# Gate products as quarter-array tiles, and three channel pairs of the output projections in float32

## The chip, the cores and the metric

The kernel runs on one core of one Trainium2 chip. The metric is the device time of one execution in microseconds (us), as the median of the runs made. Three runs of the kernel before gave 1067.7, 1067.75 and 1068.0 us. A profile holds one further execution, seen by the hardware profiler. The engines are called by short names: PE (TensorE, the matrix engine; PEld is its weight loading), DVE (VectorE), ACT (ScalarE), POOL (GpSimd) and SP (SyncE, which here issues the loads).

## What is computed

A decoder trunk of four layers on 256 tokens of width 1024, all in float32. Layers 0 and 3 mix tokens with an RG-LRU recurrence, layer 1 with a spatial gating unit, layer 2 with a short convolution, and after each of them stands a squared-ReLU MLP. The change touches the RG-LRU mixer alone:

```python
gate, xr = jnp.split(h @ w_in, 2, axis=-1)
gate = jax.nn.gelu(gate)
xr = _causal_dwconv(xr, conv_w) + conv_b
xh = xr.reshape(b, s, A_HEADS, A_HEAD_DIM)          # 16 heads of 80 channels
r = jax.nn.sigmoid(jnp.einsum("bshi,hij->bshj", xh, gate_a_w).reshape(b, s, D_RNN) + gate_a_b)
ig = jax.nn.sigmoid(jnp.einsum("bshi,hij->bshj", xh, gate_x_w).reshape(b, s, D_RNN) + gate_x_b)
log_a = -LRU_C * r * jax.nn.softplus(-lam)
a = jnp.exp(log_a)
u = jnp.sqrt(-jnp.expm1(2.0 * log_a)) * (ig * xr)
_, hs = lax.associative_scan(_lru_combine, (a, u), axis=1)
return (hs * gate) @ w_out
```

The two gates r and ig are block products: each of the 16 heads multiplies its 80 channels by its own 80 x 80 matrix, once for each gate. D_RNN is 1280, so the channels fill ten tiles of 128.

## The kernel before

Activations lie with channels on the 128 partitions and the 256 tokens along the free axis. Weights stream from memory in chunks of 128 x 2048 values, in two raw loads of 128 x 1024 (`fetch`, lines 152 to 181).

**Split products.** A large product isn't done in float32. The raw weights are cast on ACT to a rounded part `whi` (L176), DVE subtracts that from the raw ones to get `wlo` (L179), the moving side is split in the same way, and `mm3` (L240 to L243) issues three products per 128 x 128 block of weights: high by high, high by low, low by high. A few products are done in float32 from the raw weights instead, with no cast and no subtraction; the profile shows each of those as two matmul instructions. A chunk for float32 is called whole.

**The mixer of layers 0 and 3** (`class Mixer`). The program calls them layer 0 and layer 1 of this mixer, and so does this text: first mixer and second mixer. PE's order of work is `tensor_steps`, which goes through `LRU_ORDER`: the ten tiles of the recurrent branch, the ten tiles of the gated branch, and two groups of gate products ("gates", 0 and 1) between them. Then comes the output projection, five pairs of channel tiles of 32 split products' worth each (2 tiles x 8 output tiles, 48 matmuls), in the order 0 to 4 into four accumulator banks (L604 to L624). For one pair, (mixer 0, pair 1), `UNSPLIT` (L88) says that it is done in float32: two whole chunks, the recurrence output `hs` itself as moving side, L618.

The order of ACT and DVE is written out by hand in `LRU_STEPS` (L66). A word P lets PE's program run on to its next yield; C and S pop the next cast and subtraction of a weight chunk; any other word is a method of `Mixer` with a tile or pair number: x and K, k (branch and convolution), r (both gates of a tile: tanh on ACT, L714), e (exponentials, L726), da, db, dc, u, v, w, a (DVE arithmetic), s (square root, L747), z (scan, L762), g and G (gated branch and its gelu, L768 and L772), m (product of both, L776), i and o (high and low part of the result, L780 and L785). ACT and DVE work in exactly this order, each as soon as its inputs are there. PE takes an operand when it is ready and else waits with all that is behind it.

**The gates before** (`gate_steps`, L626 to L663). One group is five channel tiles with eight heads. The channels are ordered (`_rnn_order`) so that four tiles hold one whole head of 80 and 48 channels of a second one, and the fifth, called hub, holds the 4 x 32 channels left over. In one group PE does, in float32: the own product of each of the five tiles for each gate, ten of 128 x 128 (L646); the hub's share into the four tiles, 32 rows each, eight products, four of them on different row quarters of the array (L654, the tile position is the row); and the four tiles' share into the hub, eight products of 32 columns, four on different column quarters (L661). Both gates of one tile lie in one PSUM bank, so a group takes five of the eight banks. Line 714 then reads a gate of a tile in one instruction.

```python
for m in (*tiles, hub):
    banks[m] = bank().rearrange("p (j t) -> p j t", t=T)
    for e in range(2):
        nc.tensor.matmul(banks[m][:, e, :], block(), self.tile_of(m), start=e == 0, stop=False,
                         skip_group_check=True)
```

`_band_chunks` (L1038) lays the weights of a group out as 14 blocks of 128 x 128, in the order in which PE uses them, in two whole chunks of eight and six.

## Time and profile before

| | |
|---|---|
| median of three runs | 1067.75 us (1067.7 to 1068.0) |
| the profiled execution's own time | 1068.12 us |
| its span, from the first to the last instruction | 1066.1 us |
| PE busy | 1059.1 us, 99% |
| DVE busy | 725.8 us, 68% |
| ACT busy | 587.0 us, 55% |
| POOL busy | 52.5 us, 5% |
| read from memory | 200.94 MB, 189 GB/s over the span |

The span is what the trace shows; the 2.0 us between it and the execution's own time lie around it. Busy time is what instructions of an engine occupy, so for PE, whose matmuls overlap, it says only that something was under way. Start times of successive instructions tell its pace. The trace can be asked for groups of instructions by line, for one engine's instructions in order of time, for the waits, and for the chain of work that ended last.

### The profile page before, as it was taken

The numbers are of one execution on the slowest core, as the hardware profiler recorded it, in microseconds if no ns is written. First come the engines' busy times: TensorE is split into PE (matmuls) and PEld (weight loads), VectorE is DVE, ScalarE is ACT, GpSimd is POOL, SyncE is SP. The second block draws the span as 40 slices with busy tenths as digits, with TensorE's granted clock in tenths as the row PEclk, the third lists the DMA queues.
The fourth block names the chain that finished last, engine by engine and source line by source line (L and its number), as shares of the span: only waits on it lengthen the run. The fifth ranks groups of instructions, "written<-read, shape, count | busy, mean of one in ns | idle before, by whom it ended". The sixth has DMA issues, their size and how long they took to land.

```text
span 1066.1 us, 21817 instructions
## 1 busy us (share of the span) xinstructions
PE 1059.1 (99%) x9158; PEld 1046.8 (98%) x9158; DVE 725.8 (68%) x970; ACT 587.0 (55%) x819; POOL 52.5 (5%) x167
## 2 busy tenths in 40 slices
PE   9999999999999999999999999999999999999997
PEld 9999999999999999999999999999999999999997
DVE  7999765555758575555777766555578997755553
ACT  7697554454574464445544455445456975644442
POOL 3400100000210100000010010000010001000000
PEclk9999999999999999999999999999999999999999
DMA  9666585655646386665466447565554545866401
GB/s 334 254 238 213 174 279 190 194 195 190 205 162 215 98 293 196 192 194 194 155 223 198 161 138 279 195 192 189 190 179 157 175 155 181 293 192 195 131 1 41
DMA packets 58706, 203.40 MB, mean 191 GB/s; under 512 B 6640, under 2 KB 8304, under 8 KB 58608
## 3 DMA queue, kind: packets, MB, share of 16 engines
q1 hardware_dynamic: 58176, 201.49, 56.5%
q8 instruction: 72, 1.18, 0.5%
q10 hardware_dynamic: 432, 0.52, 0.1%
q14 instruction: 26, 0.21, 0.1%
HBM read 200.94 MB, written 1.05 MB: 189 GB/s over the span
## 4 chain that ended last, share of the span: by engine, by line
PE 97%; issue 2%; DVE 0%; ACT 0%; POOLq 0%; POOL 0%
PE ps L242 90%; PE ps L812 2%; PE ps L646 2%; PE ps L618 1%; PE ps L248 0%; PE ps L654 0%; PE ps L661 0%; PE ps L848 0%; PE ps L323 0%; PE ps L353 0%; DVE u L452 0%; POOLq L1139 0%; DVE lo L457 0%; POOL o L945 0%; ACT hi L454 0%
## 5 line engine op out<-in xcount | busy, mean ns | idle before, releaser
L179 DVE TENSOR_TENSOR wlo<-raw,whi 128x1024 fp32r<-128x1024 f32 (+1 forms) x378 | 440.6, 1197 | 219.5 <-ACT whi L176 219.4
L242 PE MATMUL ps<-xs,whi 128*128 128x256 f32 x3200 | 548.5, 277 | 0.0
L176 ACT CAST whi<-raw 128x1024 fp32r<-128x1024 f32 (+1 forms) x378 | 374.1, 1030 | 310.0 <-issue 286.5
L242 PEld LDWEIGHTS ps<-xs,whi 128*128 128x128 f32 x3200 | 482.9, 188 | 1.3 <-issue 0.4
L242 PE MATMUL ps<-xs,wlo 128*128 128x256 f32 x1600 | 442.0, 276 | 0.0
L242 PE MATMUL ps<-hi,whi 128*128 128x256 f32 x1296 | 357.9, 276 | 0.0
L242 PE MATMUL ps<-hi,wlo 128*128 128x256 f32 x1296 | 357.7, 276 | 0.0
L242 PE MATMUL ps<-lo,whi 128*128 128x256 f32 x1296 | 357.7, 276 | 0.0
L242 PEld LDWEIGHTS ps<-xs,wlo 128*128 128x128 f32 x1600 | 300.7, 188 | 0.0
L242 PEld LDWEIGHTS ps<-hi,whi 128*128 128x128 f32 x1296 | 243.3, 188 | 0.0
L242 PEld LDWEIGHTS ps<-lo,whi 128*128 128x128 f32 x1296 | 243.3, 188 | 0.0
L242 PEld LDWEIGHTS ps<-hi,wlo 128*128 128x128 f32 x1296 | 243.3, 188 | 0.0
L452 DVE SCALAR_TENSOR_TENSOR u<-ps,rs 128x512 f32<-128x512 f32 x64 | 44.0, 687 | 45.6 <-PE ps L242 33.2
L454 ACT ACTIVATE hi<-u 128x512 fp32r<-128x512 f32 x64 | 40.3, 630 | 16.5 <-DVE u L452 16.5
L457 DVE TENSOR_TENSOR lo<-hsq,hi 128x512 fp32r<-128x512 f32 x64 | 44.0, 688 | 4.5 <-ACT hsq L455 2.4
L281 ACT ACTIVATE xs<-x,cst 128x256 fp32r<-128x256 f32 x64 | 29.1, 501 | 30.8 <-DVE x L410 29.1
L307 POOL TENSOR_SCALAR rc<-rc 128x2 int32<-128x2 int32 x9 | 9.6, 1069 | 682.0 <-ACT rc L306 682.0
L455 ACT ACTIVATE hsq<-u 128x512 f32<-128x512 f32 x64 | 39.4, 616 | 0.0
L282 DVE SCALAR_TENSOR_TENSOR xs<-x,cst,xs 128x256 fp32r<-128x256 f32 x64 | 28.5, 480 | 12.2 <-ACT xs L281 12.2
L340 DVE TENSOR_SCALAR diag<-eye,rc 128x128 fp32r<-128x128 f32 x32 | 7.2, 285 | 29.4 <-POOL rc L330 29.4
L702 DVE SCALAR_TENSOR_TENSOR xc<-xr,cst,xc 128x255 f32<-128x255 f32 (+2 forms) x60 | 24.0, 474 | 0.0
L301 DVE TENSOR_TENSOR sum<-sum,sq 128x256 f32<-128x256 f32 x52 | 21.8, 420 | 1.4 <-ACT sq L428 0.6
(123 smaller groups left out, 478.7 us busy)
## 6 DMA issues: line engine op xcount, KB each, us to landing
raw<-weights SPq DMA_DIRECT2D x369, 512.0 KB, 4.3
raw<-first SPq DMA_DIRECT2D x16, 256.0 KB, 4.6
raw<-weights SPq DMA_DIRECT2D x4, 384.0 KB, 6.8
x<-xT SPq DMA_DIRECT2D x8, 128.0 KB, 4.4
sb<-sbias SPq DMA_DIRECT2D x2, 256.0 KB, 5.1
outT<-o SPq DMA_DIRECT2D x1, 256.0 KB, 2.1
outT<-o ACTq DMA_DIRECT2D x1, 256.0 KB, 2.1
outT<-o SPq DMA_DIRECT2D x2, 128.0 KB, 2.5
```

The costliest lines, as they stand in the source:

```text
L176: return nc.scalar.copy(out=hi[:, s], in_=raw[:, e])
L179: return nc.vector.tensor_tensor(out=lo[:, s], in0=raw[:, e], in1=hi.bitcast(F32)[:, s], op=SUB)
L242: nc.tensor.matmul(ps, a, b, start=start and n == 0, stop=stop and n == 2, skip_group_check=True)
L281: nc.scalar.activation(xs[:, hi], x, AF.Copy, scale=g)
L282: nc.vector.scalar_tensor_tensor(out=xs[:, lo], in0=x, scalar=g, in1=xs.bitcast(F32)[:, hi], op0=MULT, op1=SUB)
L301: nc.vector.tensor_tensor(out=sq_now[0], in0=sq_now[0], in1=sq[:, j, :], op=ADD)
L452: yield nc.vector.scalar_tensor_tensor(out=u, in0=ps, scalar=0.0, in1=both(scale.row), op0=MAX, op1=MULT)
L454: yield nc.scalar.activation(hi, u, AF.Square)
L455: yield nc.scalar.activation(sq, u, AF.Square)
L457: yield nc.vector.tensor_tensor(out=lo, in0=sq, in1=hi.bitcast(F32), op=SUB)
L646: nc.tensor.matmul(banks[m][:, e, :], block(), self.tile_of(m), start=e == 0, stop=False, skip_group_check=True)
L702: return [nc.vector.scalar_tensor_tensor(out=c[:, j, d:], in0=x[:, j, :T - d], scalar=self.tap(3 - d, 2 * i + j), in1=c[:, j, d:], op0=MUL ...
```

## The change

The 1280 channels are put in another order: the four tiles of a group now hold 64 channels of each of two heads (the two in the two halves of the partitions), and the hub holds the last 16 of each of the eight heads. With that an own product of one tile falls into two 64 x 64 products for each gate. The program issues the four of both gates one behind the other, on the four quarters of the array: the products of the first gate (e = 0) on the diagonal, from rows h to the same half of the output partitions, those of the second gate off it, so that the second gate's output halves lie swapped. Two tiles share two PSUM banks, one bank for each position e; a group still takes five banks. The eight products from the hub come in two parts of four, with e's bank exchanged for every second tile so that the four go to four banks. Between the two parts lie all of the hub's own products: they are now 4 x 32 columns for each gate (eight products side by side in fours), then the four tiles' share as before (eight). The second part waits for a one-element memset on POOL, `passed`, which itself waits for the first part's last product. On ACT, r now reads the second gate of the four tiles in two halves of 64 partitions, to undo the swap. A group's weights are 10 blocks in place of 14, in chunks of eight and two.

Beside that, pair 2 of the first mixer and pair 1 of the second are now done in float32 as well: three whole pairs instead of one. Their C, S, i and o steps go. In the first mixer the second group of gates now comes behind two more gated tiles, and both step lists are written anew.

```diff
--- before.py
+++ after.py
@@ -46,14 +46,14 @@
-SHARE = P // 4
+HALF, SHARE = P // 2, P // 4
 LRU_ORDER = (
     (
         ("branch", 8), ("branch", 2), ("gated", 4), ("gates", 0),
-        ("gates", 1), ("gated", 2), ("gated", 4),
+        ("gated", 2), ("gates", 1), ("gated", 4),
     ),
     (
         ("branch", 4), ("branch", 2), ("branch", 4), ("gates", 0),
@@ -64,18 +64,17 @@
 LRU_STEPS = (
...
+    "P8 na P nv P3 C P S C P S C P S C nd P C S P C S nb P S nr x0 P x1 K0 x2 P K1 x3 k0 P K2 C P k1 C P K3 P C "
+    "k2 C P C P S C x4 P C S K4 P k3 C P2 k4 P g0 P g1 r4 S P r3 S P r0 S r1 P S r2 P u0 e0 S P g2 P S e1 P da0 "
+    "u1 db0 da1 P dc0 P db1 s0 dc1 s1 P v0 v1 w0 P G0 a0 r6 w1 P z0 r8 a1 P m0 r9 z1 i0 P r7 o0 P u4 r5 u3 P G1 "
+    "u2 m1 P g3 e2 g4 P e3 P da2 db2 P dc2 e4 da3 P db3 dc3 da4 P db4 s2 dc4 s3 P v2 v3 w2 P G2 a2 w3 C z2 a3 m2 "
+    "s4 z3 P S G3 P C m3 G4 v4 i3 S P C o3 C P w4 C a4 S C P z4 C P S C P m4 C S i4 P C o4 S P C S C P S P2",
     "P4 C P C P S C S na P nv S C P S P2 C P S C nd P S nb C P nr S C P x0 P x1 K0 x2 K1 S P K2 k0 P C P C k1 P2 "
...
+    "k2 P2 x3 P x4 K3 S K4 k3 P r4 P r2 k4 P r3 r0 P S r1 P u1 C P u0 C g0 P S P S e1 P C da1 P db1 r5 S P r6 dc1 "
+    "P u2 e0 P C P da0 db0 S P s1 dc0 P s0 v1 v0 P w1 G0 w0 r8 a0 P a1 z0 C P g1 C m0 P G1 z1 i0 r7 P o0 m1 r9 P "
+    "g2 S P e2 u3 S P u4 e3 P da2 db2 P dc2 e4 g3 da3 P g4 db3 P da4 dc3 db4 s2 P s3 dc4 C v2 P v3 s4 w2 a2 P w3 "
+    "G2 z2 C P a3 G4 m2 G3 z3 P i2 C o2 m3 C P S i3 P C v4 o3 C P w4 C a4 S P C z4 P C S C P m4 S i4 P o4 P S S P "
+    "C S C P2 S P",
 )
@@ -85,7 +84,7 @@
-UNSPLIT = (0, 1)
+UNSPLIT = ((0, 1), (0, 2), (1, 1),)
 def _const_columns():
@@ -187,6 +186,12 @@
         tc.add_manual_dep(ins, other.name,
                           mybir.DependencyInfo(mybir.DependencyClass.NoSync, mybir.DependencyReason.DATA),
+                          reason="order")
+    def wait_for(ins, other):
+        tc.add_manual_dep(ins.ins, other.ins.name,
+                          mybir.DependencyInfo(mybir.DependencyClass.Sync, mybir.DependencyReason.DATA),
                           reason="order")
     def chain():
@@ -603,7 +608,7 @@
                             yield
             self.acc = [bank() for _ in range(KD // 2)]
             for i in range(KR // 2):
-                whole_pair = (self.layer, i) == UNSPLIT
+                whole_pair = (self.layer, i) in UNSPLIT
                 if whole_pair:
                     raws = [next_chunk() for _ in range(2)]
                 else:
@@ -627,6 +632,8 @@
             at, w = 0, None
             def block():
@@ -640,26 +647,50 @@
             tiles = range(g * GRP, hub)
             banks = self.banks["gates"]
-            for m in (*tiles, hub):
-                banks[m] = bank().rearrange("p (j t) -> p j t", t=T)
+            def banks_of(ms):
+                two = [bank().rearrange("p (j t) -> p j t", t=T) for _ in range(2)]
+                for i, m in enumerate(ms):
+                    banks[m] = [two[e][:, i, :] for e in range(2)]
+            for i, m in enumerate(tiles):
+                if i % 2 == 0:
+                    banks_of(tiles[i:i + 2])
+                b, x = block(), self.tile_of(m)
                 for e in range(2):
-                    nc.tensor.matmul(banks[m][:, e, :], block(), self.tile_of(m), start=e == 0, stop=False,
-                                     skip_group_check=True)
-                if m in (tiles[1], hub):
+                    for h in range(2):
+                        k, c = (slice(n * HALF, (n + 1) * HALF) for n in (h, h ^ e))
+                        nc.tensor.matmul(banks[m][e][c], b[k, c], x[k], start=i % 2 == 0, stop=False,
+                                         tile_position=(h * HALF, (h ^ e) * HALF), skip_group_check=True)
+                if i % 2:
                     yield
-            for e in range(2):
+            def from_fifth(e, ended=None):
                 b = block()
                 for i, m in enumerate(tiles):
                     q = slice(i * SHARE, (i + 1) * SHARE)
-                    nc.tensor.matmul(banks[m][:, e, :], b[q], self.tile_of(hub)[q], start=False, stop=True,
-                                     tile_position=(i * SHARE, 0), skip_group_check=True)
+                    mm = nc.tensor.matmul(banks[m][e ^ (i % 2)], b[q], self.tile_of(hub)[q], start=False, stop=True,
+                                          tile_position=(i * SHARE, 0), skip_group_check=True)
+                    if ended is not None and i == 0:
+                        wait_for(mm, ended)
+                return mm
+            seen = work.tile([1, 1], F32, name="seen", tag="seen")
+            wave = from_fifth(0)
+            passed = nc.gpsimd.memset(seen, 0.0)
+            wait_for(passed, wave)
+            ps = bank().rearrange("p (j t) -> p j t", t=T)
+            banks[hub] = [ps[:, e, :] for e in range(2)]
+            for own in (True, False):
+                for e in range(2):
+                    b = block()
+                    for i, m in enumerate(tiles):
+                        q = slice(i * SHARE, (i + 1) * SHARE)
+                        nc.tensor.matmul(banks[hub][e][q], b[:, q], self.tile_of(hub if own else m),
+                                         start=own and e == 0, stop=not own, tile_position=(0, i * SHARE),
+                                         skip_group_check=True)
             yield
-            for e in range(2):
-                b = block()
-                for i, m in enumerate(tiles):
-                    q = slice(i * SHARE, (i + 1) * SHARE)
-                    nc.tensor.matmul(banks[hub][q, e, :], b[:, q], self.tile_of(m), start=False, stop=True,
-                                     tile_position=(0, i * SHARE), skip_group_check=True)
+            from_fifth(1, passed)
             yield
         def tile_of(self, m):
@@ -711,8 +742,10 @@
             made = []
             for e, dst in enumerate((self.rg, self.ig)):
                 c = (2 * e + self.layer) * KR + m
-                made.append(nc.scalar.activation(dst[m // 2][:, m % 2, :], self.banks["gates"][m][:, e, :], AF.Tanh,
-                                                 scale=0.5, bias=half_b[:, c:c + 1]))
+                out, ps = dst[m // 2][:, m % 2, :], self.banks["gates"][m][e]
+                for h in ((slice(0, HALF), slice(HALF, P)) if e and m % GRP < GRP - 1 else (slice(0, P),)):
+                    there = h if h.stop - h.start == P else slice(HALF - h.start, P - h.start)
+                    made.append(nc.scalar.activation(out[h], ps[there], AF.Tanh, scale=0.5, bias=half_b[h, c:c + 1]))
             return made
@@ -1029,28 +1062,32 @@
     out = []
     for g in range(D_RNN // (GRP * P)):
         heads = [np.arange((g * 8 + h) * HEAD, (g * 8 + h + 1) * HEAD) for h in range(8)]
-        for i in range(GRP - 1):
-            out += [heads[i], heads[GRP - 1 + i][:P - HEAD]]
-        out += [heads[GRP - 1 + i][P - HEAD:] for i in range(GRP - 1)]
+        out += [h[:HALF] for h in heads] + [h[HALF:] for h in heads]
     return np.concatenate(out)
 def _band_chunks(gates, g):
-    own, to_four, to_fifth = [], [], []
+    own, to_four, last, to_fifth = [np.zeros((P, P), np.float32) for _ in range(GRP - 1)], [], [], []
     order = _rnn_order()[g * GRP * P:(g + 1) * GRP * P] - g * GRP * P
-    for w in gates:
+    parts = [slice(i * SHARE, (i + 1) * SHARE) for i in range(GRP - 1)]
+    halves = [slice(0, HALF), slice(HALF, P)]
+    for e, w in enumerate(gates):
         full = np.zeros((GRP * P, GRP * P), w.dtype)
         for h in range(GRP * P // HEAD):
             s = slice(h * HEAD, (h + 1) * HEAD)
             full[s, s] = w[g * GRP * P // HEAD + h]
         tiles = full[order][:, order].reshape(GRP, P, GRP, P)
-        parts = [slice(i * SHARE, (i + 1) * SHARE) for i in range(GRP - 1)]
-        own.append([tiles[m, :, m] for m in range(GRP)])
-        to_four.append(np.concatenate([tiles[-1, q, i] for i, q in enumerate(parts)], axis=0))
+        for m in range(GRP - 1):
+            for h in range(2):
+                own[m][halves[h], halves[h ^ e]] = tiles[m, halves[h], m, halves[h]]
+        to_four.append([np.roll(tiles[-1, q, i], e * HALF, axis=1) for i, q in enumerate(parts)])
+        last.append(tiles[-1, :, -1])
         to_fifth.append(np.concatenate([tiles[i, :, -1, q] for i, q in enumerate(parts)], axis=1))
-    cols = [b for pair in zip(*own) for b in pair] + to_four + to_fifth
+    rows = [np.concatenate([to_four[e ^ (i % 2)][i] for i in range(GRP - 1)]) for e in range(2)]
+    cols = own + rows[:1] + last + to_fifth + rows[1:]
     return [np.concatenate(cols[i:i + 8], axis=1) for i in range(0, len(cols), 8)]
@@ -1075,7 +1112,7 @@
                     out += _in_chunks(w, at[what], at[what] + arg * P, arg * P)
                     at[what] += arg * P
             for n, c in enumerate(_out_chunks(p["a_w_out"][j])):
-                out += unsplit([c[:, :D], c[:, D:]]) if (j, n) == UNSPLIT else [c]
+                out += unsplit([c[:, :D], c[:, D:]]) if (j, n) in UNSPLIT else [c]
         elif kind == "b":
             w = p["b_w_in"][j]
             out += _in_chunks(w, D, 2 * D) + _in_chunks(w, 0, D)
```

## Rows read from the trace of the kernel before

**Rows 1.** The page's first part, PE and DVE and ACT and POOL in one line (busy us, share of the span, instructions), and below it all the waits of PE that the trace puts down to another engine (total us, times, longest).

```profile
PE 1059.1 (99%) x9158; PEld 1046.8 (98%) x9158; DVE 725.8 (68%) x970; ACT 587.0 (55%) x819; POOL 52.5 (5%) x167
...
PE ps L248 <- DVE ones L253: 1.1, 1, 1.1
PE ps L938 <- DVE diag L935: 0.4, 1, 0.4
```

**Rows 2.** Groups of PE's instructions by line and shape over the whole run (weights rows*columns, moving shape, count | busy us, mean ns of one | idle before).

```profile
L646 PE MATMUL ps<-xc,raw 128*128 128x256 f32 x80 | 18.0, 380 | 0.0
...
L654 PE MATMUL ps<-xc,raw 32*128 32x256 f32 x64 | 4.6, 400 | 0.0
L661 PE MATMUL ps<-xc,raw 128*32 128x256 f32 x64 | 4.3, 385 | 0.0
```

**Rows 3.** Two pieces of the chain that ended last, in order of time: start us, length us, line and count of matmuls. The first is output projection in float32, the second a stretch with split products alone.

```profile
80.55 6.91 PE ps L618 x32
...
365.60 167.30 PE ps L242 x1476
```

**Rows 4.** PE in order of time across both gate groups of the first mixer: start us, us until the last of them ends, line, shapes, count.

```profile
45.44 4.48 PE L646 MATMUL ps<-xc,raw 128*128 128x256 f32 x20
49.85 1.15 PE L654 MATMUL ps<-xc,raw 32*128 32x256 f32 x16
50.92 1.07 PE L661 MATMUL ps<-xc,raw 128*32 128x256 f32 x16
51.92 4.58 PE L646 MATMUL ps<-xc,raw 128*128 128x256 f32 x20
56.44 1.15 PE L654 MATMUL ps<-xc,raw 32*128 32x256 f32 x16
57.51 1.07 PE L661 MATMUL ps<-xc,raw 128*32 128x256 f32 x16
58.51 0.51 PE L242 MATMUL ps<-xs,whi 128*128 128x256 f32 x2
```

**Rows 5.** The same for narrow windows at the start of the four-row-quarter products of the first group, up to 50.14 and then up to 50.20 us: how many had started.

```profile
49.85 0.50 PE L654 MATMUL ps<-xc,raw 32*128 32x256 f32 x4
...
49.85 0.71 PE L654 MATMUL ps<-xc,raw 32*128 32x256 f32 x8
```

**Rows 6.** PE in order of time around the first gate group of the second mixer, where the split products go on behind it.

```profile
813.67 4.48 PE L646 MATMUL ps<-xc,raw 128*128 128x256 f32 x20
818.08 1.15 PE L654 MATMUL ps<-xc,raw 32*128 32x256 f32 x16
819.15 1.07 PE L661 MATMUL ps<-xc,raw 128*32 128x256 f32 x16
...
820.15 0.50 PE L242 MATMUL ps<-xs,whi 128*128 128x256 f32 x2
```

**Rows 7.** POOL in order of time, two of its instructions on 128x2 values: the usual length and the longest.

```profile
795.26 0.20 POOL L311 TENSOR_TENSOR rc<-rc 128x2 f32<-128x2 f32 x1
...
798.34 1.25 POOL L311 TENSOR_TENSOR rc<-rc 128x2 f32<-128x2 f32 x1
```

**Rows 8.** ACT in order of time in the first mixer: start us, us, line, operation, count. Loads of a function table stand as ACT_TABLE_LOAD.

```profile
51.01 0.47 ACT L714 ACTIVATE rg<-ps,half_b 128x256 f32<-128x256 f32 x1 [5.89 <-PE ps L654]
51.38 0.47 ACT L714 ACTIVATE ig<-ps,half_b 128x256 f32<-128x256 f32 x1
...
54.59 1.15 ACT L726 ACTIVATE q<-rg,lam 128x256 f32<-128x256 f32 x2
55.58 1.14 ACT L726 ACTIVATE rg<-rg,lam 128x256 f32<-128x256 f32 x2
...
64.23 1.28 ACT L747 ACT_TABLE_LOAD   x1
65.52 1.15 ACT L747 ACTIVATE rg<-rg 128x512 f32<-128x512 f32 x2
66.69 1.28 ACT L772 ACT_TABLE_LOAD   x1
```

**Rows 9.** DVE in order of time in the first mixer, up to the finished pair 2 (its product with the gate is L776, its low part L785), and three subtractions of weights that follow each other.

```profile
81.16 0.42 DVE L758 TENSOR_SCALAR q<-q 128x512 f32<-128x512 f32 x1
81.50 0.68 DVE L751 SCALAR_TENSOR_TENSOR rg<-q,rg 128x512 f32<-128x512 f32 x1
82.10 1.26 DVE L762 TENSOR_TENSOR_SCAN rg<-q,ig 128x256 f32<-128x256 f32 x2
83.28 0.66 DVE L754 TENSOR_TENSOR ig<-ig,rg 128x512 f32<-128x512 f32 x1
83.86 0.68 DVE L776 TENSOR_TENSOR rg<-rg,gate 128x512 f32<-128x512 f32 x1
...
85.94 0.68 DVE L785 TENSOR_TENSOR lo<-rg,hi 128x512 fp32r<-128x512 f32 x1
...
97.36 3.48 DVE L179 TENSOR_TENSOR wlo<-raw,whi 128x1024 fp32r<-128x1024 f32 x3
100.77 0.68 DVE L410 TENSOR_TENSOR x<-ps,x 128x512 f32<-128x512 f32 x1
```

**Rows 10.** PE in order of time where the projection of pair 2 of the first mixer begins, behind the float32 products of pair 1.

```profile
87.11 0.47 PE L242 MATMUL ps<-hi,whi 128*128 128x256 f32 x1
```

11 rows, old and new, of the table LRU_STEPS are left out of this document.

## The prediction

> **What bounds the kernel now.** I read the page's busy times first, then PE's waits. PE is busy for 1059.1 of 1066.1 us, and all its waits for other engines are 1.5 us, at the very start and at the very end [rows 1]. Between those two ends nothing stops PE. So its time is a sum of matmuls, and an edit is worth what it takes from that sum, as long as ACT and DVE still deliver in time. Busy time can't give the price of a matmul, since they overlap: the groups show a mean of 380 ns for one of L646 [rows 2], yet twenty of them start within 4.41 us [rows 4]. So I price by starts, and by pieces of the chain divided by their count.
>
> **Prices.** A split product takes 167.30 / 1476 = 0.1133 us, a full float32 instruction 6.91 / 32 = 0.216 us [rows 3]. Instructions on different quarters of the array go side by side: after 49.85 us four start at once and the next four at about 50.17 [rows 5], and sixteen need 1.07 us [rows 4], four waves, against 16 x 0.216 = 3.45 us one by one.
>
> A change of shape costs extra. Twenty full products are 20 x 0.2155 = 4.31 us and the next shape starts after 4.41: 0.10 us for leaving. The second group's twenty need 4.52, 0.11 more, because they are entered from another shape [rows 4]. Four waves are 0.86 us; the 32-row stage takes 1.07, so 0.21 for entering and leaving, the 32-column stage 1.00, so 0.14 [rows 4]. With 0.105 for each leaving, entering is 0.105 for 32 rows and 0.03 for 32 columns.
>
> **The gates before.** One group is 4.41 + 1.07 + 1.00 us, with 0.11 for entering what follows: 6.59 us. The second mixer has the same 6.48 from 813.67 to 820.15, before that 0.11 [rows 6].
>
> **The gates after.** In waves of four instructions, each product being two instructions:
> - own products: 4 tiles x 4 quarters x 2 = 32 instructions, 8 waves
> - from the hub, first part: 4 x 2 = 8, 2 waves
> - the hub's own in 32 columns (8 x 2) and the four tiles' share (8 x 2): 8 waves
> - from the hub, second part: 2 waves
>
> That is 20 waves, 4.31 us. Shapes change five times in place of three: five leavings at 0.105 are 0.53, enterings are 0.105 twice, 0.03, 0.11 and one into 64 x 64, which the trace doesn't have. Its bounds are the neighbours, 0.03 and 0.11; I take 0.07, as 64 columns lie between 32 and 128. Sum 0.53 + 0.42 = 0.95, and a group is 5.26 us: 1.33 less, 5.3 us over four groups. If one wave could not hold four, it would be worse; a wave of all four quarters fills the array, so nothing makes it cheaper.
>
> No row shows four quarters of 64 x 64. The nearest rows are the two kinds of four side by side, by rows and by columns, both at about 0.215 a wave. The dear end is one by one as in L646. I take the cheap end because both halves of the new shape, separate row groups and separate column groups, run side by side in the rows; the next part prices the rest.
>
> **The float32 pairs.** A split pair is 48 x 0.1133 = 5.44 us, a float32 pair 32 x 0.216 = 6.91. Two more of them cost 2 x 1.47 = 2.9 us on PE. This is certain: pair 1 of the first mixer does it already.
>
> **What the other engines get.** Each such pair takes two weight subtractions from DVE, 1.14 us each (three in 100.77 - 97.36), and one o of 0.6, so 2.9 us, and from ACT two casts and one i. The gates' extra half reads give ACT 8 more instructions a mixer, 0.37 us each [rows 8], 2.9 us. The first mixer's new list also puts s4 between G2 and G3, so two more table loads of 1.3 us there [rows 8]. DVE is relieved, ACT a little more loaded, and neither sets the end by its sum. Loads shrink by four blocks a group, 1 MB in all; PE waits for no load now, so I count nothing.
>
> **The new wait.** The second hub part waits for POOL, which waits for the first part. Behind it on PE stands everything. Its cover is the hub stage between them, 8 waves and one change, 1.8 us. POOL's small instructions take 0.20 us, at worst 1.25 [rows 7]. A hand-over is short: the products of L654 end at 49.85 + 1.15 = 51.00 and ACT, which waits for them, starts at 51.01 [rows 4, 8]. With 0.1 us for two of them (my estimate from that) the wait is over after 0.3 to 1.4 us. I count nothing; with the cover gone it would cost up to 1.4 us four times.
>
> **The place without reserve.** In the first mixer the second gate group moves behind two gated tiles, so PE asks for pair 2 sooner after it. PE's clock: gates from 45.44, 5.26 us; two gated tiles 5.44; gates 5.26; four gated tiles 96 x 0.1133 = 10.9; pair 0 5.44; pair 1 6.91: pair 2 at 84.6 us. Before it was at 87.1 [rows 10], and its low part was ready at 86.6 [rows 9]. Now it needs only m2. ACT can begin r at about 49.9, when the hub stage ends. Up to s3 it has 28 gate reads (10.0 us), twenty e (9.9 at 0.495), four s and two G (6 x 0.55 = 3.3), one i (0.5), and four table loads (5.2), 28.9 us [rows 8], with about 0.8 us of gaps where s1 and i0 wait for DVE: 79.6. v can begin 0.5 earlier, after s2. Then DVE has v2, v3, w2, a2, w3, z2, a3, m2: five at 0.6, two at 0.34 and 1.18, and 0.08 until the last is through, 4.9 us [rows 9]: m2 is ready at about 84.0 to 84.5. It is 84.6 that counts: just in time. I take no stall, and keep 0 to 1.5 us for the range. The second mixer keeps its order of stages, and its pair 1 now takes PE 1.5 us longer, about what its gates save, so its pairs are asked for at nearly the old times and I count no wait there.
>
> **Sum.** -5.3 + 2.9 = -2.4 us. The profiled execution's 1068.12 us (span 1066.1 and 2.0 around it) becomes 1065.7; the median of the runs is 0.37 below that execution, so 1065.4 us.
>
> **The rivals.**
>
> *PSUM banks keep the quarters apart (slower).* The two products of one gate come from different row halves and go to the same bank, on different partitions. In the rows four row quarters write four banks (L654, a bank for each tile), and four column quarters one bank from the same rows (L661); one bank from two row halves at once is not among them. If these are held apart, a wave holds two instructions, own products need 16 waves in place of 8, 1.72 us more a group, 6.9 in all, and the kernel ends at 1065.4 + 6.9 = 1072.3 us. It decides as soon as a wave of own products takes more than 0.36 us: 32 such waves less 2.4 us are even. One by one, 24 more waves a group, it would be 20.7 us more. For it: such a form is nowhere in the trace. Against it: the partitions differ, and in L661 column quarters share a bank without loss.
>
> The Trainium skill speaks for this rival: TensorEngine Tiling (Array Packing), Restrictions and Gotchas, says under PSUM Pressure that different row tiles go to different banks and can't access the same bank at the same time. By that rule the own products would go by twos and the sum would be the rival's. The trace of before keeps to the rule everywhere, so it can't tell whether the rule holds for separate partitions too.
>
> *Pair 2 comes late (a wait for ACT or DVE takes the place of the matmuls).* If ACT runs 0.5 to 2 us behind my sum, PE stands before pair 2 of the first mixer for 0.5 to 1.5 us, and nothing behind it makes that good: 1065.9 to 1066.9, say 1066.3. For it: no reserve, two more table loads, longer gate reads. Against it: what ACT does can be added up from the rows, and the same lists now run without one wait.
>
> *The POOL wait shows.* With 1.4 us against a cover of 1.8 it doesn't. If the hand-overs and the memset took 2.1 us together, it would be 0.3 us four times, 1066.6.
>
> **How the numbers follow.** The forecast, 1065.0 to 1065.9, has 0.65; pair 2 or the POOL wait late 0.20; banks or one by one 0.15. The range 1064.7 to 1067.3 holds the first two. 0.2% of 1067.75 is 2.1 us, about what a measurement of this kernel can tell from no change, and the forecast of -2.4 lies just beyond it: of the forecast's 0.65 I give 0.47 to faster and 0.18 to same. Late cases are same, with a little for faster; slower is the bank case. Faster 0.48, same 0.38, slower 0.14.
>
> **What would show it.** Right: PE's own products of a group in starts of four, 0.215 us apart, and 1.9 us from their first start to the next shape; 1.8 us for the hub stage; 6.9 us for each of three float32 pairs; PE's waits no longer than now. Wrong: own products in twos; a wait of PE for DVE at L618 near 84 us, for POOL in the gates, or for ACT where banks come free. Any of them over 0.3 us a time ends the gain that can be measured.

## The result and the profile after

The change makes the kernel slower: 1070.68 us as the median of 12 runs (1069.32 to 1071.38), beside 1067.95 us for the kernel before on the same chip. The ratio is 1.002, 95% interval 1.0012 to 1.0028. The profiled execution took 1070.72 us, with a span of 1069.0. The prediction was 1065.4, range 1064.7 to 1067.3: wrong in sign. The runs of the change lie in two groups, five at 1069.3 to 1069.7 us with a mean granted clock of 0.999 and seven at 1070.6 to 1071.4 with 0.997, the profiled one among these.

The page's busy line after the change, as [rows 1] has it of before:

```profile
PE 1059.0 (99%) x9238; PEld 1040.5 (97%) x9238; DVE 722.3 (68%) x964; ACT 596.5 (56%) x831; POOL 53.3 (5%) x171
```

PE's waits (us in total, times, longest), as in [rows 1]:

```profile
PE ps L623 <- DVE rg L809: 2.3, 1, 2.3
PE ps L253 <- DVE ones L258: 1.1, 1, 1.1
PE ps L971 <- DVE diag L968: 0.4, 1, 0.4
PE ps L247 <- DVE lo L818: 0.3, 1, 0.3
```

PE's busy time is what it was, and two waits are new. Both stand in the output projection: L623 is the float32 pair, L809 is m, L818 is o. None is in the gates, and none for POOL.

The first gate group of the first mixer, PE in order of time (start us, us, line, shapes, count), beside [rows 4]:

```profile
44.87 1.96 PE L662 MATMUL ps<-xc,raw 64*64 64x256 f32 x32
46.76 0.71 PE L671 MATMUL ps<-xc,raw 32*128 32x256 f32 x8
47.40 1.93 PE L689 MATMUL ps<-xc,raw 128*32 128x256 f32 x32
49.27 0.71 PE L671 MATMUL ps<-xc,raw 32*128 32x256 f32 x8
49.91 0.50 PE L247 MATMUL ps<-xs,whi 128*128 128x256 f32 x2
```

The 32 instructions of the quarter products take 46.76 - 44.87 = 1.89 us, eight waves of 0.2155 with 0.16 for the changes of shape. The whole group takes 5.04 us, and with 0.09 for leaving the split products ahead of it and 0.11 for entering those behind it 5.24. The prediction had 5.26.

Where pair 2 of the first mixer begins, PE in order of time:

```profile
82.63 1.46 PE L623 MATMUL ps<-rg,raw 128*128 128x256 f32 x6
86.42 8.86 PE L623 MATMUL ps<-rg,raw 128*128 128x256 f32 x32 [2.33 <-DVE rg L809]
94.93 0.47 PE L247 MATMUL ps<-hi,whi 128*128 128x256 f32 x1
```

The last product of pair 1 starts at 83.71 and pair 2 at 86.42: 2.71 us in place of 0.22, of which 2.33 us are idle. Then pair 2 takes 94.93 - 86.42 = 8.51 us from its first product to the next kind; the same 32 instructions take 6.8 where nothing disturbs them (93.98 - 87.16 in the fill experiment below). The windows of that stretch for L623 alone show why (window, its us, PE busy and count, PEld busy and count, granted clock, DMA share, GB/s):

```profile
86.40:87.20 0.80, 0.78 (x3) 0.70 (x4) 0.92 0.59 241
87.20:90.30 3.10, 3.10 (x9) 2.42 (x8) 0.50 0.21 50
90.30:93.00 2.70, 2.70 (x14) 2.39 (x13) 0.97 0.51 159
```

From 87.2 us on the granted clock is 0.50 for some 3 us, that is 1.2 GHz in place of 2.4, and the instructions start 0.43 us apart. That costs 8.51 - 6.82 = 1.7 us more.

What made pair 2 late is on ACT. Its gate reads in the first group (start us, us, line, shapes, count), to be held against [rows 8]:

```profile
50.13 0.48 ACT L748 ACTIVATE rg<-ps,half_b 128x256 f32<-128x256 f32 x1
50.62 0.96 ACT L748 ACTIVATE ig<-ps,half_b 64x256 f32<-64x256 f32 x2
51.59 0.48 ACT L748 ACTIVATE rg<-ps,half_b 128x256 f32<-128x256 f32 x1
```

A tile with halves takes 51.59 - 50.13 = 1.46 us, each of its three reads 0.49. Priced were 0.37 a read, 1.1 a tile. Over both groups the 28 gate reads take 13.2 us, priced were 10.0. ACT was the longest part of the chain that ended in the wait; its end on DVE is m2:

```profile
85.68 0.68 DVE L809 TENSOR_TENSOR rg<-rg,gate 128x512 f32<-128x512 f32 x1
```

So m2 was done at 86.36 us. The prediction had 84.0 to 84.5, and PE asking at 84.6; PE asked at 83.9.

### The profile page after: what moved, and what is told of

The parts are those of the page before. It is cut to its first block, busy times and chain, and to the rows that moved or that the text cites. A ratio compares the mean times of both kernels' runs of the same rounds, so it can differ in the third digit from the quotient of the medians.

```text
span 1069.0 us, 21989 instructions
## 1 busy us (share of the span) xinstructions
PE 1059.0 (99%) x9238; PEld 1040.5 (97%) x9238; DVE 722.3 (68%) x964; ACT 596.5 (56%) x831; POOL 53.3 (5%) x171
## 4 chain that ended last, share of the span: by engine, by line
PE 76%; issue 16%; ACT 7%; DVE 1%; POOLq 0%; POOL 0%
PE ps L247 71%; PE ps L845 2%; ACT ig L748 1%; ACT q L759 1%; ACT rg L759 1%; PE ps L623 1%; ACT rg L748 1%; ACT whi L175 1%; ACT L780 0%; PE ps L253 0%; ACT rg L780 0%; ACT L805 0%; ACT L759 0%; PE ps L689 0%; PE ps L662 0%
## 5 line engine op out<-in xcount | busy, mean ns | idle before, releaser
L247 PE MATMUL ps<-lo,whi 128*128 128x256 f32 x1264 | 349.0, 276 | 0.3 <-DVE lo L818 0.3
L247 PE MATMUL ps<-hi,whi 128*128 128x256 f32 x1264 | 349.2, 276 | 0.0
L247 PE MATMUL ps<-hi,wlo 128*128 128x256 f32 x1264 | 348.9, 276 | 0.0
L247 PEld LDWEIGHTS ps<-lo,whi 128*128 128x128 f32 x1264 | 237.2, 188 | 0.6 <-DVE lo L818 0.5
L247 PEld LDWEIGHTS ps<-hi,whi 128*128 128x128 f32 x1264 | 237.2, 188 | 0.4 <-ACT hi L813 0.4
L247 PEld LDWEIGHTS ps<-hi,wlo 128*128 128x128 f32 x1264 | 237.2, 188 | 0.0
L623 PE MATMUL ps<-rg,raw 128*128 128x256 f32 x96 | 23.0, 401 | 2.3 <-DVE rg L809 2.3
L623 PEld LDWEIGHTS ps<-rg,raw 128*128 128x128 f32 x96 | 19.2, 202 | 5.6 <-DVE rg L809 2.7
```

Of the source, the lines that this page charges most:

```text
L247: nc.tensor.matmul(ps, a, b, start=start and n == 0, stop=stop and n == 2, skip_group_check=True)
L623: nc.tensor.matmul(o, raws[k][:, s], self.hs[i][:, k, :], start=first_in, stop=last_in, skip_group_check=True)
```

## The experiments

**Whole reads: is it the half reads?**

```diff
-                for h in ((slice(0, HALF), slice(HALF, P)) if e and m % GRP < GRP - 1 else (slice(0, P),)):
-                    there = h if h.stop - h.start == P else slice(HALF - h.start, P - h.start)
-                    made.append(nc.scalar.activation(out[h], ps[there], AF.Tanh, scale=0.5, bias=half_b[h, c:c + 1]))
+                made.append(nc.scalar.activation(out, ps, AF.Tanh, scale=0.5, bias=half_b[:, c:c + 1]))
```

> The changed kernel, but ACT reads the second gate of every tile in one instruction of 128 partitions in place of two of 64; the halves of the second gate stay swapped, so that part of the computation is changed. Theory A (the half reads make ACT late: in the changed kernel each of the eight tiles with halves takes ACT 1.47 us, where I had 1.07 and where whole reads take 0.71): PE's 2.7 us wait before pair 2 of the first mixer is gone, the half-speed stretch behind it as well, and the wait in the second mixer; the time is what the sum of the prediction gives, 1065.0 to 1065.9 us, and all runs lie within 0.5 us. Theory B (the second gate group was moved too late, or DVE is the late one): a wait of 1.5 us or more before pair 2 stays and the time is above 1067 us.

Measured: 1065.76 us (1065.55 to 1066.27), ratio to before 0.9981 (0.9972 to 0.999). PE's waits are the two of the ends again:

```profile
PE ps L253 <- DVE ones L258: 1.1, 1, 1.1
PE ps L969 <- DVE diag L966: 0.4, 1, 0.4
```

PE in order of time: both float32 pairs of the first mixer run through, 64 instructions in 13.6 us (91.0 - 77.34).

```profile
77.34 13.97 PE L623 MATMUL ps<-rg,raw 128*128 128x256 f32 x64
```

And m2 on DVE, in order of time, is done at 83.71:

```profile
83.03 0.68 DVE L807 TENSOR_TENSOR rg<-rg,gate 128x512 f32<-128x512 f32 x1
```

All of the loss hangs on the half reads. With them gone the time is the prediction's sum, and not by luck: from the last split product ahead of the gates to the first of the MLP the two mixers are 1.24 and 1.22 us shorter than before, -2.5 us against the sum's -2.4. Even so m2 is done only 0.5 us before PE asks for it, at 84.24: ACT has some 6 us less to do up to there, but now stands 2.8 us for DVE. As the halves stay where PE left them, this is a measurement and no kernel to keep.

**Which read is dear?** The r method reads some tiles in other patterns: halves that are not swapped (tile 0), the same half twice (tile 1), both gates whole (tile 3).

```diff
+                plan = {
+                    3: (((al, al),), ((al, al),)),
+                    0: (((lo, lo), (hi, hi)), ((lo, lo), (hi, hi))),
+                    1: (((al, al),), ((lo, hi), (lo, hi), (hi, lo), (hi, lo))),
...
+                for there, h in [(b, a) for a, b in plan[e]]:
```

> A probe in the changed kernel: the gate reads of single tiles are issued in different patterns, and only the distance between starts on ACT counts (parts of the gates are computed twice or with halves swapped). Tile 3: two whole reads. Tile 0: four halves, none swapped. Tile 1: one whole, then the lower output half twice and the upper one twice, all swapped. Tile 5: lower half twice, upper half twice, not swapped. Tile 6: all four pairs of halves in turn. Theory A1 (a read that follows one on another set of partitions can't overlap it): 0.36 us after a read on the same partitions, whole or half, 0.49 us after one on other partitions. Theory A2 (any read of half the partitions loses the overlap): 0.49 us for every half, also the second on the same half. Theory A3 (it is the swap, input and output on different partitions): 0.36 us for the unswapped halves of tiles 0 and 5, 0.49 for the swapped ones alone.

This is a probe: one profiled execution, and only distances between starts are read from it. ACT in order of time, tile 3 whole, tile 0 in four halves, tile 1 whole and then in halves:

```profile
50.65 0.48 ACT L755 ACTIVATE rg<-ps,half_b 128x256 f32<-128x256 f32 x1
51.01 0.48 ACT L755 ACTIVATE ig<-ps,half_b 128x256 f32<-128x256 f32 x1
51.37 0.95 ACT L755 ACTIVATE rg<-ps,half_b 64x256 f32<-64x256 f32 x2
52.33 0.95 ACT L755 ACTIVATE ig<-ps,half_b 64x256 f32<-64x256 f32 x2
53.30 0.47 ACT L755 ACTIVATE rg<-ps,half_b 128x256 f32<-128x256 f32 x1
53.80 1.96 ACT L755 ACTIVATE ig<-ps,half_b 64x256 f32<-64x256 f32 x4
```

Whole reads start 0.36 apart though each lasts 0.48, so they overlap by 0.12. Halves start 0.48 to 0.51 apart, swapped or not, so crossing partitions isn't the price. The same half twice is as slow, and from this I concluded that any read of 64 partitions gives up the overlap. That was hasty: the repeats write what the read before them wrote, and the trace has a semaphore wait on the second of each two. And one row says otherwise: the first half behind a whole read, at 51.37, comes 0.36 after it. The last experiment returns to this.

**The parts alone.** First the float32 pairs on the kernel before:

```diff
-UNSPLIT = (0, 1)
+UNSPLIT = ((0, 1), (0, 2), (1, 1))
...
```

> The kernel before with only the two further float32 pairs (pair 2 of the first mixer, pair 1 of the second): their casts, subtractions, i and o steps leave the step lists, everything else stays. By the price of the prediction PE has 2 x 1.47 us more and no wait comes up, since DVE and ACT have less to do: 1070.9 us, 0.28% over the kernel before. A rival, that float32 pairs also bring a wait of their own or a cost at the change between split and float32 products: 1071.5 us or more. Another, that they relieve DVE where it held up PE unseen: under 1070.3 us.

Measured: 1073.0 us (1072.56 to 1073.2), ratio 1.0047 (1.0035 to 1.006). The pairs cost what was priced: 13.62 us for two and 6.72 for the one of the second mixer up to the next split product, and 0.19 for entering that one. But PE now waits at the start of the MLP behind the first mixer, for xs, the split form of the residual sum x: the first 72 products there take 10.27 us in place of 8.16. Its wait:

```profile
PE ps L232 <- DVE xs L272: 1.5, 2, 1.0
```

DVE in order of time there:

```profile
95.72 8.03 DVE L169 TENSOR_TENSOR wlo<-raw,whi 128x1024 fp32r<-128x1024 f32 x7
103.67 0.69 DVE L400 TENSOR_TENSOR x<-ps,x 128x512 f32<-128x512 f32 x1
```

The pair's own subtractions are gone from the list, and seven others now stand in one row ahead of the residual sum x, in place of the four of before (three of them and x at 100.77 in [rows 9]). So the time lies 2.1 us above the 1070.9 of the price, for another reason than the rival of the expectation had. An order written by hand must be redone when an item leaves it.

Then the gates alone, in the order, lists and one float32 pair of before:

```diff
-UNSPLIT = ((0, 1), (0, 2), (1, 1),)
+UNSPLIT = ((0, 1),)
...
-        ("gated", 2), ("gates", 1), ("gated", 4),
+        ("gates", 1), ("gated", 2), ("gated", 4),
...
```

> The new gate products and half reads alone: order of stages, step lists and the one float32 pair are those of the kernel before. By PE's sum alone 1067.9 - 5.3 = 1062.6 us. By the theory that half reads make ACT late, each mixer's ACT has 8 x (1.47 - 0.71) = 6.1 us more and DVE none less, while PE asks 2.7 us sooner, and the kernel before had only 0.5 us in reserve at pair 2: waits of some 4 to 8 us in the first mixer and some in the second eat the gain, with PE at half speed behind them, 1067 to 1074 us.

Measured: 1079.59 us (1079.15 to 1080.99), ratio 1.0108 (1.0095 to 1.0122), still above the 1067 to 1074 that were expected. PE's waits:

```profile
PE ps L248 <- ACT hi L814: 9.1, 2, 5.2
```

They stand before pair 0 of both mixers: in the old order ACT does nearly all gate reads before the first pair's hi. Saved matmuls alone are worth nothing here.

**Is the rest the clock?** Eleven products of ones ahead of pair 2 in the changed kernel, so that PE doesn't stand still:

```diff
+                if (self.layer, i) == (0, 2):
+                    keep_busy(11)
```

> The changed kernel with 11 products of ones (about 2.4 us of PE's time, into a bank nobody reads) put before the projection of pair 2 in the first mixer, where PE stood for 2.7 us. Theory: the wait is ACT's and DVE's and costs the same with or without them, but PE no longer stands idle, so the stretch at half speed (matmuls 0.427 us apart from 87.2 to 90.2 us) does not come: 1069.0 to 1069.6 us in every run, as the faster ones of the changed kernel's runs, without the spread up to 1071.4. Rival: the half speed has another cause, such as slow weights or a contended memory: median 1070.5 or more and the same spread.

Measured: 1072.04 us (1071.99 to 1072.24), ratio 1.0036 (1.0023 to 1.0049). PE in order of time around pair 2:

```profile
84.68 2.62 PE L253 MATMUL ps<-ones 128*128 128x128 f32 x22
87.16 7.17 PE L625 MATMUL ps<-rg,raw 128*128 128x256 f32 x32
93.98 0.47 PE L247 MATMUL ps<-hi,whi 128*128 128x256 f32 x1
```

The window behind the ones (us, busy and count of PE, PEld, DVE, ACT and POOL, granted clock, DMA share, GB/s):

```profile
87.10:90.30 3.20, 3.20 (x17) 2.79 (x17) 3.17 (x6) 3.18 (x5) 0.00 (x0) 1.00 0.14 55
```

PE's new wait:

```profile
PE ps L247 <- DVE xs L287: 1.6, 2, 1.0
```

Pair 2 now takes 6.82 us at a clock of 1.00, and the five runs lie within 0.25 us: with PE kept busy the half speed doesn't come. The time is a miss all the same, 2.4 us above the expected 1069.0 to 1069.6. PE is 1.7 us faster up to the MLP, but the first 72 products there take 10.39 us in place of 8.16 in the change. In this run four subtractions stand ahead of x on DVE and one more between x and xs, in the change three and none; why the order differs wasn't traced.

**Halves on DVE instead.** ACT reads whole, and DVE takes its product u in halves, into a new tile:

```diff
+                for h, there in ((al, al),) if hub else ((lo, hi), (hi, lo)):
+                    made.append(nc.vector.scalar_tensor_tensor(
+                        out=self.ig[i][h, j, :], in0=swapped[there, j, :], scalar=1.0, in1=self.xc[i][h, j, :],
+                        op0=ADD, op1=MULT))
...
```

> The changed kernel with the swap undone on DVE in place of ACT: ACT reads the second gate whole (its bias is swapped to match), and u, the product with the branch, goes in halves of 64 partitions into a new tile; all else stays. By the theory that ACT's half reads alone made pair 2 late, ACT needs 0.71 us for a tile again, DVE about 2.6 us more in each mixer, in stretches where the changed kernel's DVE had gaps of 0.6 to 1.5 us: no wait before pair 2, and the time of the kernel with whole reads, 1065.8 us (1065.3 to 1066.3). Rival: DVE is nearly full there and becomes the late one: a wait of PE for DVE of 0.5 us or more, 1066.5 to 1068 us.

Measured: 1070.31 us (1068.68 to 1072.22), ratio 1.0019 (1.001 to 1.0028). PE's wait:

```profile
PE ps L623 <- DVE rg L816: 2.5, 1, 2.5
```

Two halves on DVE, in order of time:

```profile
59.40 1.39 DVE L781 SCALAR_TENSOR_TENSOR iu<-ig,xc 64x512 f32<-64x512 f32 x2
```

The halves start 0.70 apart, where whole products start 0.60 apart, and take as long as whole ones: a pair costs DVE 1.40 us in place of 0.60. DVE is as late now as ACT was. With s4 taken ahead it stays so:

```diff
...
-v2 v3 w2 P G2 a2 w3 C z2 a3 m2 s4 z3
+v2 s4 v3 w2 P G2 a2 w3 C z2 a3 m2 z3
...
```

> As the kernel with the halves on DVE, and s4 of the first mixer moved to stand with s2 and s3, which saves ACT two table loads (2.6 us) behind G2. If pair 2 is the one place without reserve, nothing is gained, 1065.8 us, for G2 comes 0.5 us later and the later pairs had time. If ACT's two loads held up pair 3 or 4, or if G2's 0.5 us is missing at pair 2, the two kernels differ by 0.3 us or more.

1069.77 us (1068.86 to 1070.97), ratio 1.0015 (1.0006 to 1.0024), PE waiting 2.6 us at the same place. The profiled execution shows something else, PE in order of time:

```profile
87.18 7.17 PE L623 MATMUL ps<-rg,raw 128*128 128x256 f32 x32 [2.58 <-DVE rg L816]
94.01 0.47 PE L247 MATMUL ps<-hi,whi 128*128 128x256 f32 x1
```

PE stood still for 2.58 us, longer than in the change, and yet pair 2 took 94.01 - 87.18 = 6.83 us, at a granted clock of 1.00 from 87 to 90 us. So standing still doesn't always bring the half speed, and a run's time hangs on whether it does.

**Halves by DMA.** ACT reads whole into an extra tile, and two transfers of 64 partitions a pair put the halves in place:

```diff
+                for h in (slice(0, HALF), slice(HALF, P)):
+                    there = slice(HALF - h.start, P - h.start)
+                    nc.gpsimd.dma_start(out=self.ig[i][h, js, :], in_=self.swapped[i][there, js, :])
...
```

> The changed kernel with the swap undone by DMA: ACT reads both gates whole (the second one's bias swapped to match), the second gate of a pair goes into an extra tile, and two transfers of 64 partitions, issued by POOL when both tiles are read, put its halves in place; DVE and ACT do nothing more than with whole reads left swapped. Theory: both engines are so full in the first mixer that the swap may cost neither of them anything; then there is no wait before pair 2 and the time is that of whole reads, 1065.8 us (1065.4 to 1066.3). Rival: the transfers land too late for u (over some 3 us after the read) or slow DVE or the weight loads: a wait at pair 2 or 0, 1067 us or more.

Measured: 1078.3 us (1076.91 to 1080.89), ratio 1.0095 (1.0081 to 1.0109). DVE waits for them:

```profile
DVE ig L784 <- DMA ig<-sw: 19.5, 6, 9.5
```

The second mixer with its old lists and without its float32 pair does no better:

```diff
-UNSPLIT = ((0, 1), (0, 2), (1, 1),)
+UNSPLIT = ((0, 1), (0, 2))
...
```

> As the kernel with the swap by DMA, and the second mixer has its old step list and its pair 1 in split products again (the first mixer keeps its three lists and two float32 pairs). By the price of a float32 pair 1.47 us less than the former, 1064.3 us, if the second mixer's ACT and DVE keep up, which were 2 us ahead of PE before; if they don't, a wait of PE at a pair of the second mixer eats part of it, 1064.8 to 1066 us.

1083.53 us (1082.42 to 1086.6), ratio 1.0148 (1.0133 to 1.0163), where 1064.3 to 1066 were expected. Then u was moved behind the transfers, directly before the product that needs it:

```diff
...
-v0 v1 w0 P
+v0 v1 u0 w0 P
...
-dc3 da4 P db4 s2 dc4 s3 P v2 v3 w2 P G2 a2 w3 C z2 a3 m2 s4 z3
+dc3 u4 da4 P db4 s2 dc4 u3 s3 P v2 u2 w2 P G2 a2 C z2 m2 v3 w3 a3 s4 z3
...
```

> ScalarE reads both gates of every tile whole, two transfers of 64 partitions per pair of tiles put the second gate's halves in place, and VectorE forms its product u for each pair as late as the chain allows (u0, u1, u2 directly before the product that takes them, u4 behind dc3, u3 behind dc4); in the first mixer pair 2's chain comes ahead of pair 3's. Theory (the time of the change is lost by reads of half the partitions alone, on ScalarE or VectorE, and everything else of it is worth what was priced): the transfers, which took some 10 us from issue to landing when u asked for them at once, now have that time, m2 of the first mixer is ready about 1 us before TensorE asks, no wait above 0.3 us stands before the output projection, and the time is 1065.5 to 1066.3 us, below the kernel before. Rival (transfers are no cheaper way, since five pairs' transfers in ten microseconds queue behind the weights): u still waits for them, TensorE waits 2 us or more for pairs 0 or 2, and the time is 1069 us or more.

1068.29 us (1067.69 to 1069.45), ratio 1.0002 (0.9993 to 1.0011): the same as before, neither of the two. The waits for transfers are gone from DVE (0.3 us left), but what they had hidden is work: three products u now stand where DVE has no free time, and m2 and pair 4's low part come late:

```profile
PE ps L238 <- DVE lo L817: 0.7, 1, 0.7
PE ps L615 <- DVE rg L808: 0.5, 1, 0.5
```

Moving two of the three, u3 and u4, behind m2 should have repaired that:

```diff
...
-dc3 u4 da4 P db4 s2 dc4 u3 s3 P v2 u2 w2 P G2 a2 C z2 m2 v3 w3 a3 s4 z3 P S G3 P C m3 G4 v4 i3 S P C o3
+dc3 da4 P db4 s2 dc4 s3 P v2 u2 w2 P G2 a2 C z2 m2 u3 v3 w3 a3 s4 z3 P G3 P m3 i3 S P C G4 o3 u4 v4 S
...
```

> As e10_dma_swap_late_u, with only the first mixer's written order changed: u3 and u4 stand behind m2 in place of ahead of it (each VectorE 0.6 us), pair 3's m, copy and remainder follow its scan at once, and the split of weights that stood ahead of pair 4's copy follows its remainder. Theory (what e10 still loses in the first mixer is order alone: m2 late by 0.5 us behind two products u that are not needed yet, pair 4's remainder late by 0.7 us behind a split of weights): m2 is done about 1.2 us earlier, both waits go, and the time falls by about 1.3 us to 1066.5 to 1067.3 us, below the kernel before by about 1 us. Rival (the transfers or their issue cost time elsewhere, by clock or by the weights' queues): the two waits go and the time stays within 0.4 us of e10, 1067.9 to 1068.7 us.

1070.3 us (1069.63 to 1071.58), ratio 1.002 (1.0011 to 1.0029): a miss for both theories. Pair 2 is in time, but pair 4 is now 1.4 us late, behind a DVE that has no idle time left there, and x follows four subtractions at 103.50 us. PE's waits and, of the stretch behind them, the window from 100 to 102 us (columns as above, the clock third from the end):

```profile
PE ps L238 <- ACT hi L812: 1.4, 1, 1.4
PE ps L238 <- DVE lo L817: 0.3, 1, 0.3
...
100.00:102.00 2.00, 2.00 (x11) 2.00 (x11) 2.00 (x3) 2.00 (x3) 0.00 (x0) 0.50 0.43 150
```

Here too the granted clock fell behind the stop, to 0.50: from 99.1 to 102.5 us the split products start 0.21 us apart in place of 0.11, which costs about 1.6 us more.

**Reads sorted by their first partition.** In the change every read of a tile with halves starts at another partition, on the input or the output side, than the read before it. Here the same reads stand in another order: of a group first all whole ones, then all lower halves (l), then all upper ones (y); in the second mixer likewise.

```diff
...
-r4 S P r3 S P r0 S r1 P S r2 P u0 e0
+r4 S P r3 S P r0 S r1 P S r2 l0 l1 l3 l2 y0 y1 y3 y2 P u0 e0
...
-m0 r9 z1 i0 P r7 o0 P u4 r5 u3 P G1 u2 m1
+m0 r9 z1 r7 r5 l8 l6 l7 l5 i0 P o0 P y8 y6 y7 y5 u4 u3 P G1 u2 m1
...
+        def l(self, m):
+            return self.gate(m, 1, slice(0, HALF), slice(HALF, P))
+        def y(self, m):
+            return self.gate(m, 1, slice(HALF, P), slice(0, HALF))
...
```

> The change with the same instructions, only ScalarE's gate reads in another order: of each group first all reads of 128 partitions (first gate, and both gates of the hub), then the second gate's lower halves (read from partition 64, written to partition 0) of all four tiles, then their upper halves (read from 0, written to 64). Theory S (the overlap with the instruction before is lost where the first partition of the input or of the output changes from one instruction to the next, not because only half the partitions take part): inside such a run of like halves starts are 0.36 us apart, each change of start costs 0.12 to 0.15 us, a group of five tiles takes about 5.4 us in place of 6.6 (first) and 7.0 (second), m2 of the first mixer is done at 83.7 to 84.3 us, the wait before pair 2 shrinks from 2.3 us to 0.4 or less with no stretch at half the granted clock, and the time is 1065.6 to 1066.6 us, below the kernel before. Theory N (any instruction on 64 partitions gives up the overlap, wherever it starts): halves stay 0.48 to 0.50 us apart, only the first gate's reads gain (8 times 0.13 us a mixer), m2 comes at 85.4 or later, the wait stays above 1.3 us, and the time is 1068.5 us or more.

Measured: 1066.53 us (1066.0 to 1067.12), ratio to before 0.9984 (0.9975 to 0.9993). That is 1.6 us below the kernel before, and 4.1 below the median of the change. ACT in order of time over the whole first group:

```profile
50.27 0.48 ACT L747 ACTIVATE rg<-ps,half_b 128x256 f32<-128x256 f32 x1 [4.68 <-PE ps L680]
50.65 0.47 ACT L747 ACTIVATE ig<-ps,half_b 128x256 f32<-128x256 f32 x1
51.00 1.57 ACT L747 ACTIVATE rg<-ps,half_b 128x256 f32<-128x256 f32 x4
52.60 3.12 ACT L747 ACTIVATE ig<-ps,half_b 64x256 f32<-64x256 f32 x8
55.75 1.09 ACT L757 ACTIVATE q<-rg,lam 128x256 f32<-128x256 f32 x2
```

PE in order of time, the end of pair 1 and pair 2 (the view ends at 91.5 us, behind 30 of its 32 instructions):

```profile
81.77 3.18 PE L614 MATMUL ps<-rg,raw 128*128 128x256 f32 x14
85.11 6.74 PE L614 MATMUL ps<-rg,raw 128*128 128x256 f32 x30 [0.15 <-DVE rg L807]
```

And m2 on DVE:

```profile
84.37 0.69 DVE L807 TENSOR_TENSOR rg<-rg,gate 128x512 f32<-128x512 f32 x1
```

Eight reads of 64 partitions take 55.75 - 52.60 = 3.15 us, 0.39 each with two changes of start in them; inside a run the trace has them 0.355 to 0.376 apart, as whole reads. The group takes 5.48 us, 6.6 in the change. So it isn't the number of partitions: the overlap goes where the first partition changes. One step bounds this, in the second group of the same mixer:

```profile
66.50 1.56 ACT L747 ACTIVATE ig<-ps,half_b 64x256 f32<-64x256 f32 x4
67.96 0.62 ACT L811 CAST hi<-rg 128x512 fp32r<-128x512 f32 x1
```

The cast reads from partition 0, the lower half ahead of it from partition 64, and still it starts 0.36 us behind that one: its input lies in SBUF, that of the reads in PSUM. m2 is done at 85.06, later than the 83.7 to 84.3 that were expected, and PE still stands idle for 0.15 us, behind which the clock stays up.

## Why the prediction was wrong

**Right: the gates.** Four quarters side by side, 0.2155 us a wave, 5.24 us a group against 5.26, 2.7 us a mixer saved. The rival of the PSUM banks is refuted: own products of one gate come from two row halves into one bank, on different partitions, and no wave was split: the four instructions of one start within 0.02 us. The rule of the Trainium skill behind that rival (TensorEngine Tiling (Array Packing), Restrictions and Gotchas, PSUM Pressure) does not show here, where the partitions differ: a wave of own products takes 0.2155 us, as any other.

**Right: the float32 pairs and "The new wait".** 6.7 to 6.9 us a pair where nothing else delays it, and no wait for POOL, whose memset takes 0.1 to 0.3 us.

**Wrong: "What the other engines get".** The half reads were priced at 0.37 us each by whole reads of [rows 8]. They and the whole reads between them take 0.49: for the eight tiles of a mixer that have halves 8 x (1.47 - 1.1) = 3 us more of ACT. The row itself had the warning: a read lasts 0.47 and the next starts after 0.37, so 0.1 of the price was overlap, and a new shape need not have it.

**Wrong: "The place without reserve".** That step had the right place and the right chain, and a reserve of 0.1 to 0.6 us, against an ACT sum that was 3 us short. m2 came at 86.36, 2 us behind the estimate, and PE asked 0.7 us earlier than estimated. The rival "Pair 2 comes late" is what happened, but it was priced at no more than 1.5 us and with one cost only. The wait was 2.5 us, and the clock took 1.7 more, which the prediction did not have at all.

The sum by PE's starts, from the last split product ahead of the gates to the first of the MLP: first mixer -2.7 (gates) + 1.5 (pair) + 2.5 (wait) + 1.7 (half speed) = +3.0, measured +3.06 (61.37 in place of 58.31). Second mixer -2.7 + 1.5 + 0.8 (pair 1 takes 0.3 us longer and the pairs behind it 0.5, with the wait at L818) = -0.4, measured -0.37 (67.33 in place of 67.70); there too the prediction counted no wait. The remaining 0.2 of the span's +2.9 us is what is left of 0.66 us less ahead of the first gates and some 0.9 more elsewhere, and wasn't traced.

That the half reads are the cause is shown twice, by whole reads (1065.76) and by sorted reads (1066.53). That the two groups of runs are runs with and without the half-speed stretch is likely, from the fill experiment, from the execution with the halves on DVE that stood still and stayed at full clock (its mean clock is 0.999), and from the clocks of the runs; but only one execution of the change was profiled.

## What to carry to other kernels

Read a price as start to start, and ask what of it is overlap with the neighbour before it is used for another shape or another start partition. Where an access must be split by partitions, sort the pieces so that those with equal starts follow each other: here this alone was worth 4.1 us. Where the engines work in orders written by hand, time saved on a full engine counts only after the orders of the others have been made to fit it.

## What the runs showed of the hardware

- **ScalarE loses its overlap where the first partition changes.** Gate reads of 128 x 256 start 0.357 us apart and last 0.47 to 0.53. Where a read's input alone moves from partition 0 to 64 (the first half behind a whole read), or its output back from 64 to 0 (a whole read behind the second half), the next start comes after 0.47 to 0.53. The Trainium skill states such a rule for VectorE (VectorE: DVE Perf Modes, Two Vector instructions with no wait between them): an instruction whose operand starts in another group of 32 partitions than the last one's in the same memory is held until everything before it has finished. VectorE's numbers here fit it: its halves start 0.70 us apart, against 0.60 for whole ones, and one lasts 0.69; no run sorts them. For ScalarE the sorted reads show the same, and the one cast that kept its overlap changed the memory as well. Only partitions 0 and 64 occur, and the bias always starts where the output does, so these two aren't told apart.
- **Half the partitions cost as much as all.** A read of 64 partitions lasts 0.46 to 0.48 us, one of 128 0.46 to 0.53.
- **A stop of TensorE can cost more than itself.** After standing 2.3 us it ran some 3 us at a granted clock of 0.50, and so it did after 1.4 us with the last of the DMA kernels. After 2.58 us in one execution, after 0.15 us idle, and with the gap filled by products of ones, it stayed at 1.00. What decides is open.
- **Transfers between partitions are slow to use.** In the first version with them VectorE waited up to 9.5 us for one transfer.
